# A long-convolution stage: split transforms against plain float32 transforms, and the order of a slot's two ways

## The chip, the cores and the metric

One core of one Trainium2 chip runs the whole program. The metric is the device time of one execution in microseconds (us). The kernel before took 4472.46 us (median of 3 runs, 4463.63 to 4475.19).

## What is computed

The program is two transformer blocks in float32 over 1024 positions and 1024 features. The change lies in the second block, in its Hyena branch:

```
z = v
for o, gate_o in enumerate((x1, x2)):
    z = gate_o * (bidirectional_long_conv(z, filters[:, o, 0], filters[:, o, 1]) + filt_bias[o] * z)
y_hy = z * jax.nn.silu(g_hy)

def bidirectional_long_conv(z, h_fwd, h_bwd):      # z: (B, L, C), h: (L, C), L = 1024
    circ = concatenate([h_fwd, zeros((1, C)), h_bwd[:0:-1]], axis=0)
    hf = rfft(circ, axis=0)
    zf = rfft(z, n=2 * L, axis=1)
    return irfft(zf * hf[None], n=2 * L, axis=1)[:, :L]
```

There are two convolutions in sequence over 512 channels, with filters that a small network makes. Beside them the second block has a wide input projection (`h @ w_in`), a windowed attention, and output projections.

## The kernel before, in words

**The transform.** A transform of length 2048 is made of two steps. A butterfly over 16 rows (8 of them zero for z) runs on VectorE (DVE) and GpSimd (POOL) in `dft16_even` and `dft16_odd`; it gives 8 *slots*, each a pair of tiles of 128x256 (real and imaginary part; the slots 0, 4, 2, 6 come from the even half, 1, 7, 3, 5 from the odd one). Then each slot is multiplied on TensorE (PE) with constant 128x128 matrices (`dft_mm`: four matrix products of 256 columns for a slot in each direction). The way back multiplies with the inverse matrices and ends in the butterfly `idft16`. Channels go in two groups g of 256, so with two orders o there are four convolutions of 8 slots.

**The split.** Before, a matrix product is three matmuls on float32r operands (a form of float32 rounded to fewer bits): `pair_split` (line 1318) rounds the pair on ScalarE (ACT, `pr_hi`, line 208) and makes the rest on POOL or DVE (`pr_lo`, line 214). The matrices, too, come in two parts; two big copies on POOL's DMA queue (`round_dft`, line 480, called in the first MLP of the program) put them into DRAM tiles of that type. Most large projections of the program (tiles `in`, `up`, `dn`) use such split products as well.

**The filter stage** (about 2864 to 3316 us). `filter_spectra` (line 1385) makes the spectra of the four filters, one call before each quarter of the projection to q, k and v: a small network (`f_ps`, plain float32 matmuls), butterflies, `flush` with 8 slots, each copied from PSUM by ACT (`spec`) and stored.

**The convolution stage** (about 3842 to 4234 us). `hyena` (line 1478) is a Python generator that yields; at 38 of its 56 yields `block2` puts in one *fill* step, 24 matmuls of the projection to the gates (tile `in`, `project_gate`). `long_conv` (line 1436) takes a slot through all of its steps: split, way there (`dft_ps`), load of the spectrum, product with the spectrum on DVE (`pt`, `pu`, lines 1456 to 1459, the last two halves on DVE or POOL), split again, a yield, way back (`idft_ps`), copy to the tile `V` by ACT. After eight slots `idft16` makes `conv_y`, the result is gated into z (`z<-conv_y,xgate`), there are four yields, and the next convolution begins with its butterflies. After each convolution of the second order, z is transposed on PE (`tp`, line 1504) and stored.

**What sets the order.** A scheduler merges the instructions into one queue for each engine, mostly as the program writes them; `high_priority` moves some ahead. An engine works its queue strictly in order. `lighter` (line 1193) puts an elementwise operation on DVE or POOL by a running sum of costs; `fma` is on DVE always. Tiles have a number of buffers (`bufs`), and a load waits on SyncE's (SP's) queue until its buffer is free.

Of the kernel before, what the change touches and what calls it, by code (L numbers as in the profile page):

```python
# [93 lines left out]
def _two_parts(x):  # L94

    def cut(v):
        m, e = np.frexp(v)
        return np.ldexp(np.rint(m * 4096), e - 12)

    hi = cut(x)  # L100
    return hi.astype(np.float32), cut(x - hi).astype(np.float32)


def _hyena_tables():
    f32 = np.float32
    c = {}
# [20 lines left out]
    for name, mats in (("dft_f", fwd), ("dft_i", inv)):  # L127
        parts = []
        for ms in mats:
            for m in ms:  # L130
                parts += list(_two_parts(m))
        c[name] = np.concatenate(parts, axis=1)
# [29 lines left out]
class Kernel:  # L162
# [317 lines left out]
    def round_dft(self, first):  # L480

        self.dft = {}
        for name in ("dft_f", "dft_i"):
            self.dft[name] = self.DR.tile([128, 50 * 128], F32R, name=name)
            self.in_order([first, self.nc.gpsimd.dma_start(self.dft[name], self.k[name])])

# [134 lines left out]
    def mlp(self, l, H, x, gate, p, close, pclose):  # L621
# [16 lines left out]
        def down_weights(c):  # L638
            dw = []
            for mt in range(2):  # L640
                n0 = c * 256 + mt * 128
                raw = pt.tile([128, 1024], F32, name="dn_raw", tag="dnr", bufs=2)
                nc.sync.dma_start(raw, down[n0 : n0 + 128, :])
                hi = p.tile([128, 1024], F32R, name="dn_hi", tag="dnh", bufs=3)
                lo = p.tile([128, 1024], F32R, name="dn_lo", tag="dnl", bufs=3)
                self.split_hi(hi, raw)
                first = self.split_lo(lo, raw, hi)
                if (l, c, mt) == (0, 4, 0):
                    self.round_dft(first)
                dw.append((hi, lo))  # L650
            return dw
# [603 lines left out]
    def idft16(self, p, v, n, y):  # L1255

        C1, C2, C3 = self.C1, self.C2, self.C3
        sub = ALU.subtract
        u = p.tile([128, 8, n], F32, name="bst", tag="bst", bufs=1)
        self.plus(u[:, 0:4], v[:, 0:4], v[:, 4:8])  # L1260
        self.plus(u[:, 4:8], v[:, 0:4], v[:, 4:8], sub)
        g = p.tile([128, 8, n], F32, name="bg", tag="bg", bufs=1)
        self.plus(g[:, 0:2], v[:, 8:10], v[:, 10:12])
        self.plus(g[:, 2:4], v[:, 8:10], v[:, 10:12], sub)
        self.plus(g[:, 4:6], v[:, 14:16], v[:, 12:14])
        self.plus(g[:, 6:8], v[:, 14:16], v[:, 12:14], sub)
# [10 lines left out]
        self.fma(y[:, 7], g[:, 1], C2, g[:, 5])  # L1277

# [16 lines left out]
    DFT_AT = {0: 0, **{d: 8 + 6 * (d - 1) for d in range(1, 8)}}  # L1295

    def dft_mats(self, p, which, d):
        n = 8 if d == 0 else 6
        m = p.tile([128, 8, 128], F32R, name="dftm", tag="dftm", bufs=2)
        at = self.DFT_AT[d] * 128  # L1300
        self.nc.sync.dma_start(m[:, :n].bitcast(F32).rearrange("p a b -> p (a b)"), self.dft[which].bitcast(F32)[:, at : at + n * 128])
# [16 lines left out]
    def pair_split(self, p, y, n):  # L1318
        hi = p.tile([128, 2, n], F32R, name="pr_hi", tag="pr_hi", bufs=2)
        lo = p.tile([128, 2, n], F32R, name="pr_lo", tag="pr_lo", bufs=2)  # L1320
        self.split_hi(hi, y)
        self.split_lo(lo, y, hi, True)
        return hi, lo
# [61 lines left out]
    def filter_spectra(self, p, o, g):  # L1385

        nc, n = self.nc, 256
        if o + g == 0:
            self.mats = p.tile([128, 50, 128], F32R, name="dftf")
# [22 lines left out]
        def flush(ds):  # L1412
            for d in ds:
                yy = self.pair_split(p, slots[d], n)
                if o + g == 0:
                    r = slice(self.DFT_AT[d], self.DFT_AT[d] + (6 if d else 8))
                    nc.sync.dma_start(self.mats[:, r].bitcast(F32).rearrange("p a b -> p (a b)"),
                                      self.dft["dft_f"].bitcast(F32)[:, r.start * 128 : r.stop * 128])
                ps = self.PS.tile([128, 2, n], F32, name="dft_ps", tag="sm", bufs=2)
                self.dft_mm(ps, self.mats[:, self.DFT_AT[d] :], yy, n, d)  # L1420
# [13 lines left out]
    V_AT = {0: (14, 15), 1: (0, 2), 2: (8, 9), 3: (1, 3), 4: (12, 13), 5: (5, 7), 6: (10, 11), 7: (4, 6)}  # L1434

    def long_conv(self, p, z, o, g):

        nc, n = self.nc, 256
        v = p.tile([128, 16, n], F32, name="V", tag="V", bufs=1)
        slots = {}  # L1440

        def Y(d):
            slots[d] = p.tile([128, 2, n], F32, name="Y", tag="Y", bufs=4)
            return slots[d]

        def through(ds):
            for d in ds:
                yy = self.pair_split(p, slots[d], n)
                m = self.dft_mats(p, "dft_f", d)
                ps = self.PS.tile([128, 2, n], F32, name="dft_ps", tag="sm", bufs=2)  # L1450
                self.dft_mm(ps, m, yy, n, d)
                h = p.tile([128, 3, n], F32, name="spec", tag="spec", bufs=1)
                nc.sync.dma_start(h, self.specd[o, g, d])
                t = p.tile([128, 2, n], F32, name="pt", tag="pt", bufs=1)
                u = p.tile([128, 2, n], F32, name="pu", tag="pu", bufs=1)
                nc.vector.tensor_mul(t, ps, h[:, 0:2])
                nc.vector.tensor_mul(u, ps, h[:, 1:3])
                self.plus(t[:, 0], t[:, 0], t[:, 1], ALU.subtract)
                self.plus(t[:, 1], u[:, 0], u[:, 1])
                gg = self.pair_split(p, t, n)  # L1460
                m = self.dft_mats(p, "dft_i", d)
                yield
                ps = self.PS.tile([128, 2, n], F32, name="idft_ps", tag="sm", bufs=2)
                self.dft_mm(ps, m, gg, n, d)
                a, b = self.V_AT[d]
                nc.scalar.activation(v[:, a : b + 1 : b - a], ps, AF.Copy)

        self.dft16_even(p, z, n, Y)
        yield
        yield from through((0, 4, 2, 6))  # L1470
        self.dft16_odd(p, z, n, Y)
        yield
        yield from through((1, 7, 3, 5))
        y = p.tile([128, 8, n], F32, name="conv_y", tag="conv_y", bufs=1)
        self.idft16(p, v, n, y)
        return y

    def hyena(self, hy, zd, xgd, yhd):
        nc, i = self.nc, self.i
# [6 lines left out]
        for o in range(2):  # L1486
            for g in range(2):
                ch = slice(g * 256, g * 256 + 256)
                y = yield from self.long_conv(hy, z[g], o, g)
                b = fb[:, o, ch].unsqueeze(1).to_broadcast([128, 8, 256])  # L1490
                for c in (slice(0, 4), slice(4, 8)):
                    self.plus(z[g][:, c], z[g][:, c], b[:, c], ALU.mult)
                    self.plus(y[:, c], y[:, c], z[g][:, c])
                for a in range(0, 8, 2):
                    gt = hy.tile([128, 2, 256], F32, name="xgate", tag="xgate", bufs=2)
                    nc.sync.dma_start(gt, xgd[o, a : a + 2, :, ch].rearrange("a p c -> p a c"))
                    self.plus(z[g][:, a : a + 2], y[:, a : a + 2], gt, ALU.mult)
                for _ in range(4):
                    yield
                for cc in range(2 if o else 0):  # L1500
                    for hf in range(2):
                        tp = self.PS.tile([128, 4, 128], F32, name="tp2", tag="sm", bufs=2)
                        for a in range(4):
                            nc.tensor.transpose(tp[:, a], z[g][:, 4 * hf + a, cc * 128 : cc * 128 + 128], self.ident)
                        t = hy.tile([128, 512], F32, name="zt", tag="zt", bufs=1)
                        nc.scalar.activation(t, tp.rearrange("p a b -> p (a b)"), AF.Copy)
                        nc.scalar.dma_start(yhd[2 * g + cc, hf], t)
# [37 lines left out]
    def block2(self, _, H, xs, close):  # L1545
# [45 lines left out]
        with self.pool("hyena", "right") as hy:  # L1591

            for n, _ in enumerate(self.hyena(hy, zd, xgd, yhd)):
                if (n + 1) * 38 // 56 > n * 38 // 56:
                    next(fill)
# [409 lines left out]
```

## Time and profile before

| | |
|---|---|
| median of 3 runs | 4472.46 us |
| the profiled execution | 4475.41 us, its span 4473.6 us |
| PE busy | 4130.8 us (92%) |
| DVE, ACT, POOL busy | 2082.0 (47%), 1488.5 (33%), 1488.1 us (33%) |
| DMA | 471.21 MB, mean 105 GB/s |
| mean granted clock of PE | 0.963 of full |

How to read it: a busy share is the time in which at least one instruction of the engine is in flight; matmuls overlap, so one of 392 ns can follow another after 228 ns. PEclk is the granted clock of PE as a share of the full 2.4 GHz; its other level is 0.5 (1.2 GHz). A plain float32 matmul stands in the trace as two records with the same names, a float32r one as one record. Waits are idle time of an engine ahead of an instruction, with the instruction that ended it.

### The profile page before, as it was taken

How to read it: one execution, taken by the hardware profiler on the slowest of the kernel's cores; microseconds unless marked ns; L12 is line 12 of the kernel's file. 1: busy time of each engine (PE TensorE's matmuls, PEld its weight loads, DVE VectorE, ACT ScalarE, POOL GpSimd, SP SyncE). 2: the span in 40 equal slices, each digit the busy share in tenths (PEclk: the TensorE clock that was granted, in tenths of full speed). 3: DMA queues.
4: the chain of work that ended last, by engine and by line, in shares of the span. 5: the costliest groups of instructions: out<-in, count | busy, mean ns of one | idle time of the engine just before them, and what ended most of it. 6: DMA issues, size and time to landing. Idle time of an engine off the chain costs nothing. (4 is left out here: it accounts for less than half of the span.)

```text
span 4473.6 us, 53257 instructions
## 1 busy us (share of the span) xinstructions
PE 4130.8 (92%) x20132; PEld 3220.5 (72%) x20132; DVE 2082.0 (47%) x3791; ACT 1488.5 (33%) x2822; POOL 1488.1 (33%) x1349
## 2 busy tenths in 40 slices
PE   6999888999999899888999999899999999877998
PEld 4776666888886686676888887567777676766777
DVE  6336675332335516586233324642322443577546
ACT  5435444212123515445212121323224444222222
POOL 3322455333333412254433332131230111355342
PEclk8999899999999999899999999999999999998999
DMA  6245533221111135623211111344453321645563
GB/s 195 62 134 164 166 121 92 92 61 52 47 51 58 47 106 180 202 93 116 74 44 52 43 52 48 105 123 104 113 145 83 90 86 48 188 150 157 164 193 113
DMA packets 566388, 471.21 MB, mean 105 GB/s; under 512 B 197416, under 2 KB 460670, under 8 KB 566002
## 3 DMA queue, kind: packets, MB, share of 16 engines
q1 hardware_dynamic: 375514, 367.43, 27.0%
q10 hardware_dynamic: 189880, 92.63, 7.2%
q0 software_dynamic: 736, 7.73, 0.5%
q8 instruction: 159, 2.61, 0.2%
q14 instruction: 99, 0.81, 0.1%
HBM read 364.17 MB, written 107.47 MB: 105 GB/s over the span
## 5 line engine op out<-in xcount | busy, mean ns | idle before, releaser
L214 POOL TENSOR_TENSOR w_lo<-w_raw,w_hi 128x1024 fp32r<-128x1024 f32 (+4 forms) x222 | 411.0, 1852 | 1015.8 <-ACT w_hi L208 936.4
L205 PE MATMUL dn<-act,dn_hi 128*128 128x512 f32 x2048 | 636.5, 392 | 9.8 <-ACT act L208 4.2
L662 DVE SCALAR_TENSOR_TENSOR xa<-dn,mod,xa 128x512 f32<-128x512 f32 x512 | 383.9, 750 | 277.8 <-PE dn L205 276.0
L205 PE MATMUL in<-b2h,w_hi 128*128 128x512 f32 x1152 | 467.3, 406 | 5.5 <-ACT qkv_t L1626 5.5
L205 PE MATMUL in<-b2h,w_lo 128*128 128x512 f32 x1152 | 466.6, 405 | 0.0
L205 PE MATMUL in<-b2l,w_hi 128*128 128x512 f32 x1152 | 466.3, 405 | 0.0
L208 ACT ACTIVATE w_hi<-w_raw 128x1024 fp32r<-128x1024 f32 (+4 forms) x276 | 236.8, 859 | 683.1 <-PE in L205 249.2
L205 PEld LDWEIGHTS dn<-act,dn_hi 128*128 128x128 f32 x2048 | 386.1, 189 | 95.1 <-ACT act L208 5.3
L205 PE MATMUL up<-fh,w_hi 128*128 128x512 f32 x1024 | 405.9, 396 | 0.7 <-DVE relu L632 0.4
L205 PE MATMUL up<-fl,w_hi 128*128 128x512 f32 x1024 | 402.9, 393 | 1.9 <-POOL fl L214 1.5
L205 PE MATMUL up<-fh,w_lo 128*128 128x512 f32 x1024 | 404.0, 395 | 0.0
L205 PE MATMUL dn<-act,dn_lo 128*128 128x512 f32 x1024 | 401.0, 392 | 2.8 <-POOL dn_lo L214 2.8
L632 DVE TENSOR_TENSOR relu<-up,relu 128x512 f32<-128x512 f32 x128 | 88.4, 691 | 604.5 <-ACT relu L631 604.5
L214 POOL TENSOR_TENSOR dn_lo<-dn_raw,dn_hi 128x1024 fp32r<-128x1024 f32 x64 | 151.9, 2392 | 524.5 <-ACT dn_hi L208 524.5
L205 PEld LDWEIGHTS in<-b2h,w_hi 128*128 128x128 f32 x1152 | 225.4, 196 | 57.4 <-issue 8.5
L205 PEld LDWEIGHTS in<-b2h,w_lo 128*128 128x128 f32 x1152 | 225.2, 195 | 51.6 <-issue 7.3
L205 PEld LDWEIGHTS in<-b2l,w_hi 128*128 128x128 f32 x1152 | 225.1, 195 | 50.0 <-issue 6.2
L208 ACT ACTIVATE dn_hi<-dn_raw 128x1024 fp32r<-128x1024 f32 x64 | 64.7, 1052 | 553.4 <-PE dn L205 546.1
L214 POOL TENSOR_TENSOR act<-relu,act 128x512 fp32r<-128x512 f32 x128 | 167.7, 1311 | 190.4 <-ACT act L208 190.3
L205 PEld LDWEIGHTS up<-fl,w_hi 128*128 128x128 f32 x1024 | 192.5, 188 | 49.0 <-POOL fl L214 3.2
L205 PEld LDWEIGHTS up<-fh,w_hi 128*128 128x128 f32 x1024 | 192.4, 188 | 46.6 <-issue 1.4
L205 PEld LDWEIGHTS up<-fh,w_lo 128*128 128x128 f32 x1024 | 192.6, 188 | 45.5 <-issue 1.0
(502 smaller groups left out, 8349.0 us busy)
## 6 DMA issues: line engine op xcount, KB each, us to landing
wada<-in_w_ada SPq DMA_DIRECT2D x120, 512.0 KB
w_raw<-in_w_in SPq DMA_DIRECT2D x102, 512.0 KB
w_raw<-in_w_mlp_up SPq DMA_DIRECT2D x64, 512.0 KB
dn_raw<-in_w_mlp_down SPq DMA_DIRECT2D x64, 512.0 KB
qkv<-qkv_t ACTq DMA_DIRECT2D x72, 256.0 KB
w_raw<-in_w_out SPq DMA_DIRECT2D x64, 256.0 KB
mix<-mix SPq DMA_DIRECT2D x64, 256.0 KB
spectra<-spec ACTq DMA_DIRECT2D x32, 384.0 KB
```

Of the source, the lines that this page charges most:

```text
L205: return self.nc.tensor.matmul(out, lhsT, rhs, start=start, stop=stop, **kw)
L208: self.nc.scalar.activation(hi, x, AF.Copy, **kw)
L214: return eng.tensor_sub(lo, x, hi.bitcast(F32))
L632: nc.vector.tensor_mul(sq, ps, sq)
L662: nc.vector.scalar_tensor_tensor(x[f, hf], ps, gate[:, f : f + 1], x[f, hf], op0=ALU.mult, op1=ALU.add)
```

## The change

1. Matrices and pairs are plain float32. `pair_split`, `round_dft` and the two-part matrices go; a product is one matmul, its matrix is loaded from the constants (192 KB in place of 384 KB for a slot).
2. `long_conv` goes. `hyena` runs over all 32 slots of the four convolutions in one sequence: way there of slot j (`slot_there`, with the product with the spectrum, all on DVE and at high priority), a yield, way back of slot j-1 (`slot_back`, with its own PSUM tag `im`). `idft16` is cut in two, the even half after four slots, the odd half after the first slot of the next convolution. The next convolution's butterflies are made while the slots of the present one run.
3. The fill steps are paced anew: 34 over the first 32 yields, then one at each. The buffers of matrices (2 to 5), spectra (1 to 2), `pt` (1 to 2) and slots (4 to 6) grow.

```diff
-    def dft_mm(self, ps, m, y, n, d):
-
-        yh, yl = y
+    def dft_mm(self, ps, m, y, d):
+
         if d == 0:
             terms = (((0, 0), (1, 1)), ((2, 0), (3, 1)))
         else:
             terms = (((0, 0), (2, 1)), ((1, 0), (0, 1)))
         for o in range(2):
-            k = 0
-            for mat, part in terms[o]:
-                for a, b in ((2 * mat, yh), (2 * mat, yl), (2 * mat + 1, yh)):
-                    self.mm(ps[:, o], m[:, a], b[:, part], k == 0, k == 5)
-                    k += 1
...
+            for k, (mat, part) in enumerate(terms[o]):
+                self.mm(ps[:, o], m[:, mat], y[:, part], k == 0, k == 1)
...
+    def slot_there(self, p, y, o, g, d):
...
+        m = self.dft_mats(p, "dft_f", d)
+        ps = self.PS.tile([128, 2, n], F32, name="dft_ps", tag="sm", bufs=2)
+        self.dft_mm(ps, m, y, d)
+        h = p.tile([128, 3, n], F32, name="spec", tag="spec", bufs=2)
+        nc.sync.dma_start(h, self.specd[o, g, d])
+        t = p.tile([128, 2, n], F32, name="pt", tag="pt", bufs=2)
+        u = p.tile([128, 2, n], F32, name="pu", tag="pu", bufs=1)
+        with self.tc.high_priority():
+
+            nc.vector.tensor_mul(t, ps, h[:, 0:2])
+            nc.vector.tensor_mul(u, ps, h[:, 1:3])
+            nc.vector.tensor_sub(t[:, 0], t[:, 0], t[:, 1])
+            nc.vector.tensor_add(t[:, 1], u[:, 0], u[:, 1])
+            self.load[0] += 0.84
+        return t, self.dft_mats(p, "dft_i", d)
+
+    def slot_back(self, p, t, m, v, d):
+
+        ps = self.PS.tile([128, 2, 256], F32, name="idft_ps", tag="im", bufs=2)
+        self.dft_mm(ps, m, t, d)
+        a, b = self.V_AT[d]
+        self.nc.scalar.activation(v[:, a : b + 1 : b - a], ps, AF.Copy)
...
+        for j in range(len(seq) + 1):
+            if j < len(seq):
+                k, half, at, d = seq[j]
+                on_way[j] = self.slot_there(hy, ready.pop((k, d)), *divmod(k, 2), d)
+            yield
+            if j == 0:
+                continue
+
+            k, half, at, d = seq[j - 1]
...
+            self.slot_back(hy, *on_way.pop(j - 1), V[half], d)
+            if (half, at) == (0, 0) and k:
+                self.idft16_odd(hy, V[1], n, y)
+                gating(k - 1, y)
+            if (half, at) == (0, 1):
+                self.dft16_odd(hy, z[k % 2], n, slots(k))
+            if (half, at, k) == (0, 2, 3):
+                features_first(0)
+            if (half, at) == (1, 0):
+                y = hy.tile([128, 8, n], F32, name="conv_y", tag="conv_y", bufs=1)
+                self.idft16_even(hy, V[0], n, y)
+            if (half, at) == (1, 1) and k < 3:
+                self.dft16_even(hy, z[1 - k % 2], n, slots(k + 1))
+        self.idft16_odd(hy, V[1], n, y)
+        gating(3, y)
+        for _ in range(3):
+            yield
+        features_first(1)
```

**The order on PE.** Between two slots, before in the first convolution and now at the start of the second (line 205 is the matmul helper, in the changed kernel line 191). Before:

```order
L205 MATMUL in_29577<-b2h_1_21970,w_hi 128x512
L205 MATMUL idft_ps<-pr_hi,dftm 128x256
L205 MATMUL in_29577<-b2l_1_21971,w_hi 128x512
L205 MATMUL in_29577<-b2h_1_21970,w_lo 128x512
L205 MATMUL dft_ps<-pr_hi,dftm 128x256
L205 MATMUL idft_ps<-pr_lo,dftm 128x256
L205 MATMUL idft_ps<-pr_hi,dftm 128x256 x2
L205 MATMUL idft_ps<-pr_lo,dftm 128x256
```

and now, one row with x4 being all products of a slot in one direction:

```order
L191 MATMUL in_29254<-b2l_1_21977,w_hi 128x512
L191 MATMUL in_29254<-b2h_1_21976,w_lo 128x512
L191 MATMUL idft_ps<-pt,dftm 128x256 x4
L191 MATMUL dft_ps<-Y,dftm 128x256 x4
L191 MATMUL in_29355<-b2h_0_21701,w_hi 128x512
L191 MATMUL in_29355<-b2l_0_21702,w_hi 128x512
```

Before, the first `pr_hi` matmul of a slot stands ahead of its `pr_lo` ones, and fill and two slots mix. Now all four products of one slot's way back stand together with the next but one slot's way there, and 24 fill matmuls stand between such visits.

**The order on DVE.** From the first convolution into the second (`z_29048`, now `z_28660`, is z of the first channel group, `z_29050`, now `z_28662`, of the second; lines 1204 and 1208 are elementwise helpers, now 1181 and 1185; 1418 to 1421 are the product with the spectrum; 1677, now 1675, ends a gate). Before:

```order
L1204 TENSOR_TENSOR conv_y<-conv_y,bst 128x256
L1208 SCALAR_TENSOR_TENSOR conv_y<-bpq,conv_y 128x256 x12
L1204 TENSOR_TENSOR bst<-z_29050 128x1024
L1677 SCALAR_TENSOR_TENSOR gate_t<-in_29842,b_in,gate_t 128x512
L1204 TENSOR_TENSOR conv_y<-conv_y,z_29048 128x1024
L1204 TENSOR_TENSOR z_29048<-conv_y,xgate 128x512
L1204 TENSOR_TENSOR Y<-bst 128x512
L1204 TENSOR_TENSOR Y<-bst 128x256
L1204 TENSOR_TENSOR bmn<-bst 128x256 x2
L1208 SCALAR_TENSOR_TENSOR Y<-bmn,bst 128x256
L1677 SCALAR_TENSOR_TENSOR gate_t<-in_29957,b_in,gate_t 128x512
L1208 SCALAR_TENSOR_TENSOR Y<-bmn,bst 128x256
```

and now:

```order
L1185 SCALAR_TENSOR_TENSOR conv_y<-bpq,conv_y 128x256 x5
L1418 TENSOR_TENSOR pt<-dft_ps,spec 128x512
L1419 TENSOR_TENSOR pu<-dft_ps,spec 128x512
L1420 TENSOR_TENSOR pt<-pt 128x256
L1181 TENSOR_TENSOR conv_y<-conv_y,z_28660 128x1024
L1421 TENSOR_TENSOR pt<-pu 128x256
L1181 TENSOR_TENSOR z_28660<-conv_y,xgate 128x512
L1181 TENSOR_TENSOR bpq<-z_28662 128x256 x5
L1185 SCALAR_TENSOR_TENSOR bst<-bpq,z_28662 128x256 x2
L1675 SCALAR_TENSOR_TENSOR gate_t<-in_29355,b_in,gate_t 128x512
L1181 TENSOR_TENSOR z_28660<-conv_y,xgate 128x512
L1185 SCALAR_TENSOR_TENSOR bst<-bpq 128x256 x2
```

Before, the next convolution's first slots (`Y`) come behind the whole way out of the last one (`conv_y`, `z`). Now that way out stands between the spectrum products of the next convolution's first slots, and ahead of the butterflies of its odd half (`bpq<-z`).

## Rows read from the trace of the kernel before

**Rows 1.** View of stretches: start:end, length, busy us (instructions) of each engine

```profile
core 0: us, PE busy (x) PEld busy (x) DVE busy (x) ACT busy (x) POOL busy (x), PEclk, DMA share, GB/s
870.00:890.00 20.00, 20.00 (x89) 16.37 (x88) 3.77 (x6) 5.42 (x7) 8.30 (x6) 1.00 0.67 234
2864.00:3316.00 452.00, 418.57 (x1849) 326.94 (x1848) 168.32 (x268) 127.47 (x263) 129.30 (x84) 0.95 0.43 120
3842.20:4233.80 391.60, 321.93 (x1666) 265.37 (x1667) 267.21 (x400) 99.52 (x155) 191.76 (x135) 0.91 0.53 164
```

**Rows 2.** The same view, at a change of convolution and at the stage's end

```profile
3900.00:3950.00 50.00, 35.96 (x175) 29.27 (x173) 39.08 (x51) 9.19 (x14) 30.50 (x22) 0.86 0.45 139
...
4215.00:4230.00 15.00, 6.56 (x24) 4.50 (x23) 6.69 (x3) 2.83 (x4) 7.25 (x4) 0.66 0.49 155
```

**Rows 3.** Waits of TensorE (PE), convolution stage: us in total, times, longest us

```profile
PE dft_ps L205 <- ACT pr_hi L208: 22.9, 2, 11.5
PE tp L1504 <- POOL z L1204: 20.6, 4, 11.1
PE idft_ps L205 <- ACT pr_hi L208: 11.7, 11, 2.7
```

**Rows 4.** Waits of PE, filter stage, 2864 to 3316 us

```profile
PE dft_ps L205 <- POOL pr_lo L214: 13.7, 9, 4.5
PE dft_ps L205 <- ACT pr_hi L208: 8.4, 5, 3.8
```

**Rows 5.** View of stretches for tile `in` alone, convolution stage: the projection's matmuls

```profile
3842.20:4233.80 391.60, 218.86 (x866) 162.89 (x867) 7.43 (x10) 24.39 (x36) 0.91 0.53 164
```

**Rows 6.** Groups of PE in the convolution stage: shapes, count | busy us, mean ns

```profile
L205 PE MATMUL dft_ps<-pr_hi,dftm 128*128 128x256 f32 x256 | 57.9, 304 | 28.9 <-ACT pr_hi L208 22.9 <-DMA dftm<-dft_f 5.9
...
L1504 PE MATMUL tp<-ident,z 128*128 128x128 f32 x32 | 7.5, 356 | 22.8 <-POOL z L1204 20.6 <-DVE z L1204 2.2
```

**Rows 7.** Timeline of PE, 4195 to 4200 us: start us, length us, engine, line, tiles, count

```profile
4195.28 0.40 PE L205 MATMUL in<-b2l,w_hi 128*128 128x512 f32 x1
...
4197.79 0.39 PE L205 MATMUL in<-b2h,w_hi 128*128 128x512 f32 x1
...
4199.15 0.40 PE L205 MATMUL idft_ps<-pr_hi,dftm 128*128 128x256 f32 x2
...
4200.34 0.39 PE L205 MATMUL in<-b2l,w_hi 128*128 128x512 f32 x1
```

**Rows 8.** Timeline of PE, 2837 to 2845 us: plain float32 matmuls of 512 columns

```profile
2837.45 7.13 PE L205 MATMUL ms<-nsq,ones_d 128*128 128x512 f32 x16
...
2844.65 0.39 PE L205 MATMUL in<-b2h,w_lo 128*128 128x512 f32 x1
```

**Rows 9.** Timeline of PE, 2998 to 3003 us: plain float32 matmuls of 256 columns

```profile
2998.10 4.95 PE L205 MATMUL f_ps<-fw,fhid 64*128 64x256 f32 x20
3002.98 0.50 PE L205 MATMUL in<-b2h,w_hi 128*128 128x512 f32 x1
```

**Rows 10.** Timeline of VectorE (DVE), 3914 to 3956 us: from one convolution into the next

```profile
3914.67 1.23 DVE L1204 TENSOR_TENSOR bst<-V 128x1024 f32<-128x1024 f32 x1 [2.62 <-ACT V L1466]
...
3922.74 6.30 DVE L1208 SCALAR_TENSOR_TENSOR conv_y<-bpq,conv_y 128x256 f32<-128x256 f32 x12
...
3930.76 2.70 DVE L1204 TENSOR_TENSOR conv_y<-conv_y,z 128x1024 f32<-128x1024 f32 x1
3933.39 2.83 DVE L1204 TENSOR_TENSOR z<-conv_y,xgate 128x512 f32<-128x512 f32 x1
...
3944.64 2.43 DVE L1204 TENSOR_TENSOR bpq<-z 128x256 f32<-128x256 f32 x3
...
3954.62 0.74 DVE L1208 SCALAR_TENSOR_TENSOR Y<-bst 128x256 f32<-128x256 f32 x2
```

**Rows 11.** Groups of GpSimd (POOL) in the convolution stage

```profile
L214 POOL TENSOR_TENSOR pr_lo<-Y,pr_hi 128x512 fp32r<-128x512 f32 x30 | 45.3, 1509 | 97.2 <-ACT pr_hi L208 88.8 <-DMA dftm<-dft_f 5.0 <-DMA spec<-spectra 3.4
```

**Rows 12.** Groups of DVE in the convolution stage

```profile
L1456 DVE TENSOR_TENSOR pt<-dft_ps,spec 128x512 f32<-128x512 f32 x32 | 22.0, 688 | 39.4 <-PE dft_ps L205 37.7 <-issue 1.4
```

More of the change, by code (lines that the diff above doesn't have):

```diff
@@ L127, in _hyena_tables @@
     for name, mats in (("dft_f", fwd), ("dft_i", inv)):
[L128 to L132, printed above, removed]
+        c[name] = np.concatenate([m for ms in mats for m in ms], axis=1).astype(np.float32)
     L, E, bands = S, 33, 16
@@ L646, in down_weights @@
                 self.split_hi(hi, raw)
-                first = self.split_lo(lo, raw, hi)
-                if (l, c, mt) == (0, 4, 0):
-                    self.round_dft(first)
+                self.split_lo(lo, raw, hi)
                 dw.append((hi, lo))
@@ L1277, in idft16, with idft16_odd @@
         self.fma(y[:, 7], g[:, 1], C2, g[:, 5])
+    def idft16_odd(self, p, v, n, y):
+        C1, C2, C3 = self.C1, self.C2, self.C3
+        sub = ALU.subtract
+        u = p.tile([128, 8, n], F32, name="bst", tag="bst", bufs=1)
+        self.plus(u[:, 0:4], v[:, 0:4], v[:, 4:8])
+        self.plus(u[:, 4:8], v[:, 0:4], v[:, 4:8], sub)
         w = p.tile([128, 6, n], F32, name="bpq", tag="bpq", bufs=1)
@@ L1293, in idft16 @@
                 self.fma(y[:, b], w[:, a - 1], sg * cp, y[:, b])
-    DFT_AT = {0: 0, **{d: 8 + 6 * (d - 1) for d in range(1, 8)}}
+    DFT_AT = {0: 0, **{d: 4 + 3 * (d - 1) for d in range(1, 8)}}
     def dft_mats(self, p, which, d):
-        n = 8 if d == 0 else 6
-        m = p.tile([128, 8, 128], F32R, name="dftm", tag="dftm", bufs=2)
+        n = 3 if d else 4
+        m = p.tile([128, 4, 128], F32, name="dftm", tag="dftm", bufs=5)
         at = self.DFT_AT[d] * 128
-        self.nc.sync.dma_start(m[:, :n].bitcast(F32).rearrange("p a b -> p (a b)"), self.dft[which].bitcast(F32)[:, at : at + n * 128])
+        self.nc.sync.dma_start(m[:, :n].rearrange("p a b -> p (a b)"), self.k[which][:, at : at + n * 128])
         return m
-    def dft_mm(self, ps, m, y, n, d):
-        yh, yl = y
+    def dft_mm(self, ps, m, y, d):
         if d == 0:
@@ L1432, in filter_spectra @@
         flush((1, 7, 3, 5))
-    V_AT = {0: (14, 15), 1: (0, 2), 2: (8, 9), 3: (1, 3), 4: (12, 13), 5: (5, 7), 6: (10, 11), 7: (4, 6)}
-    def long_conv(self, p, z, o, g):
+    V_AT = {0: (6, 7), 1: (0, 2), 2: (0, 1), 3: (1, 3), 4: (4, 5), 5: (5, 7), 6: (2, 3), 7: (4, 6)}
+    def slot_there(self, p, y, o, g, d):
         nc, n = self.nc, 256
[L1439 to L1476, printed above, removed]
@@ L1485, in hyena @@
             nc.sync.dma_start(z[g], zd[g].rearrange("a p c -> p a c"))
[L1486 to L1507, printed above, removed]
@@ new lines, in hyena, with slots, Y, gating @@
+        ready = {}
+        def slots(k):
+            def Y(d):
+                ready[k, d] = hy.tile([128, 2, n], F32, name="Y", tag="Y", bufs=6)
+                return ready[k, d]
+            return Y
+        def gating(k, y):
+            o, g = divmod(k, 2)
+            ch = slice(g * 256, g * 256 + 256)
+            b = fb[:, o, ch].unsqueeze(1).to_broadcast([128, 8, 256])
+            for c in (slice(0, 4), slice(4, 8)):
+                self.plus(z[g][:, c], z[g][:, c], b[:, c], ALU.mult)
+                self.plus(y[:, c], y[:, c], z[g][:, c])
+            for a in range(0, 8, 2):
+                gt = hy.tile([128, 2, 256], F32, name="xgate", tag="xgate", bufs=2)
+                nc.sync.dma_start(gt, xgd[o, a : a + 2, :, ch].rearrange("a p c -> p a c"))
+                self.plus(z[g][:, a : a + 2], y[:, a : a + 2], gt, ALU.mult)
@@ new lines, in features_first @@
+        def features_first(g):
+            for cc in range(2):
+                for hf in range(2):
+                    tp = self.PS.tile([128, 4, 128], F32, name="tp2", tag="sm", bufs=2)
+                    for a in range(4):
+                        nc.tensor.transpose(tp[:, a], z[g][:, 4 * hf + a, cc * 128 : cc * 128 + 128], self.ident)
+                    t = hy.tile([128, 512], F32, name="zt", tag="zt", bufs=1)
+                    nc.scalar.activation(t, tp.rearrange("p a b -> p (a b)"), AF.Copy)
+                    nc.scalar.dma_start(yhd[2 * g + cc, hf], t)
@@ new lines, in hyena @@
+        self.dft16_even(hy, z[0], n, slots(0))
+        seq = [(k, half, at, d) for k in range(4) for half, ds in enumerate(((0, 4, 2, 6), (1, 7, 3, 5))) for at, d in enumerate(ds)]
+        V, y, on_way = {}, None, {}
+        for j in range(len(seq) + 1):
[6 more added lines that the diff above has]
+            k, half, at, d = seq[j - 1]
+            if at == 0:
+                V[half] = hy.tile([128, 8, n], F32, name=f"V{half}", tag=f"V{half}", bufs=1)
+            self.slot_back(hy, *on_way.pop(j - 1), V[half], d)
[11 more added lines that the diff above has]
+                self.dft16_even(hy, z[1 - k % 2], n, slots(k + 1))
@@ L1593, in block2 @@
             for n, _ in enumerate(self.hyena(hy, zd, xgd, yhd)):
-                if (n + 1) * 38 // 56 > n * 38 // 56:
+                if n >= 32 or (n + 1) * 34 // 32 > n * 34 // 32:
+                    next(fill)
+                if n < 32 and (n + 1) * 34 // 32 > n * 34 // 32 + 1:
                     next(fill)
```

44 lines of the change are left out of this document (11 added, 33 removed).

## Prediction

> **What bounds the kernel now.** I read the view of stretches first. In the convolution stage TensorE (PE) is busy 321.9 of 391.6 us, DVE 267.2 and POOL 191.8 [rows 1]: PE bounds, but stands idle for 69.7 us, and its mean granted clock is 0.91, so about 18% of the stage went at the lower of the two levels, half speed. In the filter stage it is busy 418.6 of 452.0 us at 0.95 [rows 1]. The idle time is not spread evenly. Where one convolution gives way to the next, PE is busy 36.0 of 50 us while DVE is busy 39.1, and at the stage's end 6.6 of 15 us at a clock of 0.66 [rows 2]. The waits say for what: 22.9 us in only two waits for `pr_hi` of a new convolution's slot, 20.6 us for the finished z ahead of the transposes, 11.7 us in small waits for `pr_hi` between the two ways of a slot [rows 3]. In the filter stage it is the split again, 13.7 us for `pr_lo` and 8.4 us for `pr_hi` [rows 4].
>
> How much is to be had? PE's work without any wait has a floor. 866 fill matmuls [rows 5] follow one another after (4197.79 - 4195.28) / 11 = 0.228 us [rows 7]: 197.4 us. A float32r matmul of 256 columns takes (4200.34 - 4199.15) / 10 = 0.119 us [rows 7]; a slot has 12 in each direction, 768 in all (256 of them in the row shown, [rows 6]): 91.4 us. With the transposes' 7.5 us [rows 6] the floor is 296.3 us. So 391.6 - 296.3 = **95.3 us** of this stage are waits and half speed. The change can win there, and nowhere else as much.
>
> **The products themselves** get dearer. A plain float32 product is two records in the trace. Sixteen of 512 columns and one fill matmul fill 7.20 us [rows 8], so a record takes (7.20 - 0.23) / 16 = 0.436 us, and of 256 columns half, 0.218: 0.436 us for a product, against 3 x 0.119 = 0.357 before. The other bound are records of 256 columns that use only 64 rows of the array: 4.88 / 20 = 0.244 us [rows 9], 0.488 for a product. I take 0.436, from full 128x128 matrices like these. The 256 products of the convolutions then take 111.6 us in place of 91.4, +20.2 us. Entering a run of plain products costs some 0.1 us more ([rows 9] stand 0.5 us above 20 x 0.218; with four records to an entry that is five entries); 33 visits: +3.3 us. Page "FP8 and Floating Point Precision" of the Trainium skill, section "TensorE Precision Notes", says that true float32 takes four passes through the array. By that a product would be an estimated 4 x 0.119 = 0.476 us, 15.4 us more over all 384 products than by my price; [rows 8] lie below it and are nearer to this use.
>
> **The order** pays for that. What is late next? Between the two ways of a slot now stand another slot's products and 24 fill matmuls, 5.5 us, against a spectrum product of four DVE instructions (0.69 us for each of the two wide ones [rows 12], some 2.2 us together): the small waits go, and `pr_hi`, `pr_lo` go with the split. At a change of convolution the way out of the old one (`idft16_odd`, gating) now runs under the new one's even slots, whose `Y` were made during the old one. Late next are then the odd slots. Their chain on DVE is: `bst` to the end of `conv_y`, 3914.67 to 3929.0, 14.4 us; gating, 2.70 + 2.83 = 5.5 us; butterflies from `bpq` to the first odd `Y`, 3944.64 to 3955.4, 10.7 us [rows 10]; two spectrum products, 4.4 us. That is 35.0 us. But these DVE instructions ran beside a busy POOL at up to twice their usual length (the twelve `conv_y` here 0.52 us apart; the same width costs 0.37 us in the last of [rows 10]), and POOL loses 45.3 us of `pr_lo` [rows 11]. I take 30 us. The cover is three slot steps from the last way back to the first odd way there, each 24 x 0.228 + 8 x 0.436 + 0.1 = 9.1 us: 27 us. So 3 us of waiting stay at each of three changes, and some 2 us of half speed behind them: 15 us. At the start the first four slots stand close together with little fill between them, after a wait for z that stays: 8 us. At the end the last way out (14.4 + 5.5 us) has three fill steps of 16.4 us as cover: 4 us of waiting and 4 of half speed. Together 31 us of the 95.3 stay.
>
> Convolution stage after: 296.3 + 20.2 + 3.3 + 31 = 350.8 us, against 391.6: **-41 us**.
>
> **The filter stage.** 128 products, each 0.079 dearer: +10 us, and some 24 entries, +2. The 22.1 us of waits for the split [rows 4] have no split to wait for any more; but slots stand closer together now, and the DVE butterflies feed them, so I count three quarters, 17 us, as gone: **-5 us**. Bounds: +12 with nothing won, -20 with all of it and the half speed behind it.
>
> **What costs nothing.** The two copies of `round_dft` go; PE was busy 20.00 of the 20 us around them [rows 1], so nothing waited. ACT loses 96 `pr_hi`, and is no bound at 99.5 us. DVE gains the spectrum product's last halves that POOL shared, and loses its share of `pr_lo`; at 267 of 391.6 us [rows 1] it has room. On SP's queue the matrices stand behind the gating's loads (`xgate`), which wait for z; with five buffers they are two and a half slots, 22 us, ahead, more than the gating's 5.5 us. Matrix loads halve; the waits for them are not among those shown. POOL's queue holds `w_lo` of the fill between butterflies, as before. If that cover fails, odd slots come later, which is the third rival.
>
> **Sum.** -41 - 5 = -46 us on the profiled execution's 4475.4 us (span 4473.6); it stands 3 us above the median of the runs, so **4427 us**. A measurement tells no change from one within 0.3%, 13 us.
>
> **Rivals.**
> - *All waits go* (14%). DVE's instructions shorten to their undisturbed length, the chain falls to 25 us and is covered, the filter stage gives 20 us: 4427 - 15 - 5 - 15 = 4392 us. For it: DVE loses work and POOL 45 us. Against it: start and end stay as they are.
> - *The dear product* (10%): a product costs 0.488 us, as in [rows 9], 384 x 0.052 = +20 us: 4447 us. Against it speaks [rows 8]. By the four passes of the Trainium skill's page it would be an estimated 4442 us.
> - *The butterflies take the wait's place* (5%, slower). DVE works in order, and the spectrum products, put ahead, hold up the butterflies whenever PE is late, while the way out waits for POOL's half of `bst<-V`, queued behind a `w_lo`. Each us of the chain beyond 27 costs 3 us, once per change. From a chain of 50 us on, the kernel is slower than the bound; at 52 us it gives 4427 + 3 x 22 + 3 = 4496 us. Before, the chain with a busy POOL was 35.0 us [rows 10], so much more than that is needed.
> - *No difference* (9%): the dear product, the chain at its full 35.0 us with 12 us lost at each change (+21), together 4427 + 20 + 21 = 4468 us. That the way back does not stand behind the next slot is excluded by the order on PE.
>
> **How the numbers follow.** The forecast keeps 62%. Its own range, 4408 to 4446, is the chain between 27 and 33 us and the filter stage's bounds. The range of 8 in 10 reaches down to the first rival, 4392, and up to 4460, where the no-difference case begins. Faster by over 13 us: forecast, first and second rival, 0.86; same 0.09; slower 0.05.
>
> **What would show it.** In the profile after: two records of about 0.22 us pitch for a product, 512 records each for `dft_ps` and `idft_ps` in the stage; its length near 351 us; PE's waits for `pr_hi` and `pr_lo` gone, small waits for `Y` at the first odd slot of a convolution, a wait for z of some 4 us before the last transposes; PEclk up from 0.91 towards 0.96. It is wrong if PE waits more than 10 us for `Y` at each change, if records lie 0.24 us apart, or if the stage of attention or the end moves, where PE's order is the same.

## The result and the profile after

The changed kernel takes **4432.24 us** (median of 4 runs, 4425.2 to 4444.01), the kernel before 4469.45 us in runs on the same chip: a ratio of 0.9919, 95% interval 0.9894 to 0.9945. A second measurement gave 0.992 (0.990 to 0.9941). The forecast was 4427 us. The profiled execution of the changed kernel is the slowest of its four, 4444.01 us with a span of 4442.2 us, so the two traces differ by 31 us, the medians by 37.

The view of stretches of the changed kernel: start:end, length, busy us (instructions) of each engine, PEclk, DMA share, GB/s. First the convolution stage, then the stretch from the last score product of the attention to the last transpose, then six us behind a wait.

```profile
3843.10:4202.80 359.70, 325.91 (x1414) 272.18 (x1415) 238.56 (x373) 64.06 (x92) 150.98 (x98) 0.94 0.46 143
...
3769.30:4202.60 433.30, 394.12 (x1748) 327.88 (x1748) 258.73 (x403) 85.21 (x124) 165.60 (x107) 0.95 0.45 139
...
3951.70:3957.70 6.00, 6.00 (x14) 4.78 (x15) 6.00 (x11) 0.00 (x0) 1.41 (x2) 0.51 0.63 200
```

The convolution stage fell from 391.6 us [rows 1] to 359.7, PE's idle time in it from 69.7 to 33.8 us, and PEclk rose from 0.91 to 0.94. What is left of the waits (waits of PE in the stage: us in total, times, longest us; the last of them, for a load, ends at the stage's first product and so lies just ahead of it):

```profile
PE dft_ps L191 <- issue: 16.4, 2, 11.2
PE tp L1467 <- DVE pu L1419: 6.7, 1, 6.7
PE idft_ps L191 <- DVE pt L1420: 4.4, 1, 4.4
PE tp L1467 <- DVE z L1181: 3.4, 2, 2.2
PE tp L1467 <- POOL z L1181: 2.7, 2, 2.0
PE dft_ps L191 <- DMA dftm<-const_dft_f: 2.6, 1, 2.6
```

Nothing waits for `pr_hi` or `pr_lo` any more [rows 3]. The two waits whose releaser is not named (11.2 and 5.2 us) stand ahead of the first odd slot of the second and of the third convolution. DVE shows what they were: the matmul follows the start of its `Y` by half a microsecond at both (3951.70 after 3951.19, 4036.78 after 4036.26). The timeline of DVE at the first:

```profile
3919.54 0.43 DVE L1185 SCALAR_TENSOR_TENSOR bpq<-bst 128x256 f32<-128x256 f32 x1 [2.28 <-POOL bst L1181]
...
3922.64 2.58 DVE L1185 SCALAR_TENSOR_TENSOR bpq<-bst 128x256 f32<-128x256 f32 x1
...
3930.49 0.68 DVE L1418 TENSOR_TENSOR pt<-dft_ps,spec 128x512 f32<-128x512 f32 x1
...
3943.04 2.88 DVE L1185 SCALAR_TENSOR_TENSOR bst<-bpq 128x256 f32<-128x256 f32 x2
3945.84 2.89 DVE L1185 SCALAR_TENSOR_TENSOR bst<-bpq,z 128x256 f32<-128x256 f32 x2
...
3951.19 2.75 DVE L1185 SCALAR_TENSOR_TENSOR Y<-bst 128x256 f32<-128x256 f32 x8
```

and the timelines of PE and of POOL (same columns):

```profile
3867.27 1.89 PE L191 MATMUL idft_ps<-pt,dftm 128*128 128x256 f32 x8
3869.00 1.89 PE L191 MATMUL dft_ps<-Y,dftm 128*128 128x256 f32 x8
3876.19 1.89 PE L191 MATMUL idft_ps<-pt,dftm 128*128 128x256 f32 x8
...
3951.70 3.75 PE L191 MATMUL dft_ps<-Y,dftm 128*128 128x256 f32 x8 [11.23 <-issue]
```

```profile
3914.59 4.92 POOL L1181 TENSOR_TENSOR bst<-V 128x1024 f32<-128x1024 f32 x2 [8.16 <-ACT V L1430]
...
3922.40 2.54 POOL L200 TENSOR_TENSOR w_lo<-w_raw,w_hi 128x1024 fp32r<-128x1024 f32 x1
...
3930.38 2.41 POOL L1181 TENSOR_TENSOR conv_y<-conv_y,z 128x1024 f32<-128x1024 f32 x1 [5.44 <-DVE conv_y L1185]
...
3942.52 3.12 POOL L1181 TENSOR_TENSOR bg<-V 128x512 f32<-128x512 f32 x2
3945.60 2.52 POOL L200 TENSOR_TENSOR w_lo<-w_raw,w_hi 128x1024 fp32r<-128x1024 f32 x1
```

Eight records take 3869.00 - 3867.27 = 1.73 us, so a plain product of two records takes 0.432 us. A slot step takes 3876.19 - 3867.27 = 8.92 us. The chain from `bst` (on POOL now) to the first odd `Y` takes 3951.5 - 3914.6 = 37 us, and PE had work for 26 of them. After the wait PE works at the lower level of its clock for 6 us (0.51), in the other rows of the stage it is mostly at the higher.

**Where the 31 us of the two traces come from.** I cut both at the same four instructions. The first cut is a sum ahead of the filter stage (`ms<-nsq`, at 2837.45 us [rows 8] and 2850.29), behind the same PE work in both. Up to it: +12.8 us; from there to the first score product of the attention (the filter stage): 560.8 to 548.4, **-12.4**; attention: 366.7 to 370.7, +4.0; from the last score product to the last transpose: 468.7 to 433.3, **-35.4**; the rest: -0.4. The filter stretch in four kernels, two with the split (before, and `order_alone` below) and two without (changed, and `odd_first` below):

```profile
2837.45:3398.24 560.79, 521.82 (x2282) 409.20 (x2281) 190.39 (x294) 166.35 (x342) 139.86 (x89) 0.95 0.44 119
...
2841.24:3396.40 555.16, 513.72 (x2284) 403.61 (x2283) 192.59 (x294) 166.58 (x342) 140.95 (x89) 0.97 0.45 121
...
2850.29:3398.64 548.35, 518.89 (x2154) 406.06 (x2153) 164.41 (x275) 148.89 (x310) 105.19 (x76) 0.97 0.44 117
...
2848.79:3396.40 547.61, 517.75 (x2156) 405.84 (x2155) 164.41 (x275) 148.61 (x310) 105.16 (x76) 0.97 0.44 117
```

Over all profiles of this study it takes 555.1 to 560.8 us in the four kernels with the split and 547.1 to 548.7 in the ten profiles without: the filter stage did gain. But half or more of that is lost just ahead of it. The last stretch of the first block (from its last 128 `dn` matmuls to `ms<-nsq`) takes 64.3 to 66.2 us with the split and 70.0 to 71.7 without. PE's order differs there. Before, `dn` follows the last `ms<-nacc`; now the block's last five `up` matmuls stand between them:

```profile
2809.94 2.03 PE L205 MATMUL ms<-nacc,ones_d 128*128 128x512 f32 x2 [2.89 <-POOL nacc L1541]
2810.98 1.84 PE L205 MATMUL dn<-act,dn_hi 128*128 128x512 f32 x2
...
2815.26 2.08 PE L191 MATMUL ms<-nacc,ones_d 128*128 128x512 f32 x2 [1.10 <-POOL nacc L1537]
2816.35 1.42 PE L191 MATMUL up<-fl,w_hi 128*128 128x512 f32 x1
```

Why the scheduler orders it so, and whether that order is what costs the time, was not tried. The attention has the same work in both, and over the profiles of this study it took 354 to 373 us: its +4.0 is the spread of single executions. The gain that stays is nearly all the convolution stage's.

### The profile page after: what moved, and what is told of

The parts are those of the page before. It is cut to its first block, busy times and chain, and to the rows that moved or that the text cites. A ratio compares the mean times of both kernels' runs of the same rounds, so it can differ in the third digit from the quotient of the medians.

```text
span 4442.2 us, 52202 instructions
## 1 busy us (share of the span) xinstructions
PE 4143.3 (93%) x19748; PEld 3232.0 (73%) x19748; DVE 2024.9 (46%) x3742; ACT 1434.8 (32%) x2726; POOL 1416.9 (32%) x1300
## 5 line engine op out<-in xcount | busy, mean ns | idle before, releaser
L200 POOL TENSOR_TENSOR w_lo<-w_raw,w_hi 128x1024 fp32r<-128x1024 f32 (+4 forms) x236 | 445.4, 1888 | 1119.4 <-ACT w_hi L194 1027.7
L194 ACT ACTIVATE w_hi<-w_raw 128x1024 fp32r<-128x1024 f32 (+4 forms) x276 | 236.8, 859 | 749.3 <-PE in L191 316.3
L191 PEld LDWEIGHTS dn<-act,dn_lo 128*128 128x128 f32 x1024 | 194.1, 190 | 44.9 <-POOL dn_lo L200 3.6
```

Source lines behind the costliest of these rows:

```text
L191: return self.nc.tensor.matmul(out, lhsT, rhs, start=start, stop=stop, **kw)
L194: self.nc.scalar.activation(hi, x, AF.Copy, **kw)
L200: return eng.tensor_sub(lo, x, hi.bitcast(F32))
```

## The experiments

For each kernel, "stretch" is the time from the last score product to the last transpose in its profile (before 468.7 us with PE idle for 77.6; changed 433.3 with 39.2). It begins ahead of the stage, since in some of these kernels the stage's first slots are interleaved with the attention's last work. "The order" in the runs below includes the change's new pacing of the fill, which no run tries by itself.

### The plain products alone

```diff
 # the kernel before, dft_mm, dft_mats and filter_spectra as in the change
-                yy = self.pair_split(p, slots[d], n)
...
-                gg = self.pair_split(p, t, n)
```

> The kernel before, in its own order, with the plain float32 products of the change and without the splits. Theory (the order brings the gain of the convolution stage): the filter stage shortens by about 12 us as in the changed kernel (its code is the same), and in the convolution stage 20 to 25 us of dearer products eat most of the 35 us of waits for the split, since each slot's way back still waits for its own spectrum product: stage 380 to 392 us, whole 4445 to 4460 us. Rival (the gain comes from dropping the split, in whatever order): stage about 360 us, whole about 4432 us, as the changed kernel. A third: the dear products dominate, stage over 400 us, whole above 4465 us.

Measured: 4449.72 us, ratio 0.9946 (0.9928 to 0.9964); stretch 451.6 us. The whole time is as the theory had it. In its profile the filter stretch shortened by 13.7 us (560.8 to 547.1), much as expected, and the stretch by 17.1, while the rest of the program took some 3 us more. The waits of PE in its convolution stage:

```profile
PE idft_ps L191 <- POOL pt L1181: 19.8, 13, 14.3
PE tp L1467 <- POOL z L1181: 14.5, 4, 8.7
PE dft_ps L191 <- POOL Y L1181: 7.8, 1, 7.8
```

The waits for `pr_hi` [rows 3] go without any new order. That is worth more than the dearer products cost: PE's idle time in the stretch falls by 23.1 us (77.6 to 54.5), and its busy time rises by only 6.0 (391.1 to 397.1) instead of 20, at a granted clock of 0.94 in place of 0.92.

### The order alone

```diff
 # the changed kernel, dft_mm and the matrices as in the kernel before
-        self.dft_mm(ps, m, y, d)
+        self.dft_mm(ps, m, self.pair_split(p, y, n), n, d)
...
-        return t, self.dft_mats(p, "dft_i", d)
+        return self.pair_split(p, t, n), self.dft_mats(p, "dft_i", d)
```

> The order of the change with the three float32r products of the split, of the kernel before, in both stages (matrices in two buffers and one buffer of spectra, for want of room). Theory (order): the filter stage stays at its 563 us, and the convolution stage falls to 345 to 370 us, 20 us less of products than the changed kernel but with ACT's and POOL's splits back between the spectrum product and the way back, which the next slot's way there now hides: whole 4425 to 4450 us. Rival (dropping the split is what counts): waits for the split's high and low part come back, stage 385 us or more, whole 4465 us or more.

Measured: 4486.81 us, ratio 1.0032 (1.0021 to 1.0043), slower than before by 0.3%; stretch 485.8 us. PE waited 44.1 us there for loads of matrices, since only two buffers had room: no fair trial of the order. This kernel and the next two also keep one buffer of `pt` and of spectra, where the change has two. With three buffers of matrices:

> The order of the change with the split products, as in order_alone, but with three buffers of matrices instead of two (the first slot's two extra matrices in a tile of their own; five buffers of Y instead of six pay for it). In order_alone TensorE waited 44.1 us for the loads of matrices. From the last score product of the attention to the last transpose the stretches are 468.8 us in the kernel before, 451.5 with the plain products alone, 433.3 in the changed kernel. Theory (order and plain products each take a part of the waits): the loads' waits go, stretch 440 to 452 us, whole 4437 to 4455 us. Rival (under this order the split itself is on the path: POOL's low parts queue behind butterflies on POOL): stretch 455 to 470 us, whole 4455 to 4475 us.

Measured: 4482.37 us, ratio 1.002 (1.0007 to 1.0034); stretch 481.4 us. The rival came out, and more: the loads' waits went, and the split's came in their place.

```profile
PE dft_ps L205 <- POOL pr_lo L214: 43.4, 24, 5.1
```

As written, the split of slot j+1's `Y` stands behind the split of slot j's spectrum on ACT and POOL, so the way there of j+1 waits for the whole way of j's data: the order hides little. So I wrote it earlier:

```diff
         self.dft_mm(ps, m, y, n, d)
+        ahead()                    # the split of slot j+1, in its own pair of buffers
```

> order_alone_3bufs with the split of the next slot's Y written ahead of the spectrum product of this slot, in a pair of buffers of its own, so that on ACT and POOL it no longer stands behind the split of the spectrum. In order_alone_3bufs TensorE waited 43.4 us in 24 waits for POOL's low part ahead of the way there. Theory (that place in the written order is what cost the order its gain): those waits go, the stretch from the last score product to the last transpose falls from 481.4 us to 435 to 455 us, whole 4435 to 4455 us. Rival (POOL, with splits and butterflies, is late in any order): stretch 465 us or more, whole 4465 us or more.

Measured: 4461.54 us, ratio 0.9987 (0.9971 to 1.0003); the profiled execution is the fastest of its ten, 4446.03 us, with a stretch of 453.8 us. It lies 15.5 us below the median; outside the stretch it took 3990.5 us, the least of all profiles here (the others take up to 4013.8), so a part of the 15.5 us lies there, and a part may lie in the stretch. `pr_lo` holds the way there for 10.1 us instead of 43.4:

```profile
PE dft_ps L205 <- ACT pr_hi L208: 15.5, 3, 5.9
PE idft_ps L205 <- POOL pr_lo L214: 11.3, 6, 2.7
PE dft_ps L205 <- POOL pr_lo L214: 10.1, 3, 4.4
```

So the place of the split cost the order alone a good part of what it lost (the two intervals of the ratio do not overlap); the profile's stretch is in the theory's range, the median between theory and rival. By the ratios the products alone give 24 us, the order alone costs 9 us as written and gives some 6 us (-1 to 13, so perhaps nothing) with the split early, both together 36. The two parts are not a sum: the plain product is dearer for PE, and it takes the split out of the order's way.

### What the priority does

```diff
-        with self.tc.high_priority():
```

> The changed kernel without the higher priority of the spectrum product, so that VectorE may run butterflies that were written earlier ahead of it. Theory (a slot's way back has some 7 us of cover, the next way there and the fill, and a burst of butterflies is 8 to 30 us): waits of TensorE for pt come at the four or more bursts, 10 to 40 us in all, whole 4443 to 4470 us. Rival (the scheduler places it in time anyhow, or the waits only change place with those for the odd slots): 4425 to 4438 us.

> The changed kernel unaltered, beside the other runs of this call, to tell their differences from the chip's. All theories: 0.9895 to 0.9945 of the kernel before, about 4433 us.

Measured: without the priority 4434.86 us, 0.9921 (0.990 to 0.9943), stretch 433.4 us; the changed kernel beside it 4438.61 us, 0.992. The rival: the priority gives nothing.

### The chain at a change of convolution

```diff
-            if (half, at) == (0, 0) and k:
-                self.idft16_odd(hy, V[1], n, y)
-                gating(k - 1, y)
-            if (half, at) == (0, 1):
-                self.dft16_odd(hy, z[k % 2], n, slots(k))
+            if (half, at) == (0, 0):
+                self.dft16_odd(hy, z[k % 2], n, slots(k))
+            if (half, at) == (0, 1) and k:
+                self.idft16_odd(hy, V[1], n, y)
+                gating(k - 1, y)
```

> The changed kernel with the odd half of the transform there written ahead of the odd half of the transform back and the gating at each change of convolution. Theory (what is left of TensorE's idle time is that chain of 37 us against 27 us of cover): the waits of 11.2 and 5.2 us ahead of the first odd slot go, with part of the half speed behind them: convolution stage 337 to 347 us, whole 4410 to 4420 us. Rival (the same work only comes later: the gated input of the next convolution but one, or the last slots, wait in its place): stage 355 to 365 us, whole 4427 to 4440 us.

Measured: 4420.66 us, 0.9879 (0.9851 to 0.9907), stretch 420.6 us, PE idle in it for 25.8 us in place of 39.2. Repeated:

> odd_first unaltered, for a narrower interval of the version that has been fastest. All theories: 0.986 to 0.990 of the kernel before, about 4422 us, below the changed kernel's 0.990 to 0.994.

Measured: 4424.81 us, 0.9898 (0.9878 to 0.9917), stretch 421.1 us. The theory: the 16.4 us of waits ahead of odd slots are gone, and the stage, 347.1 us, and the whole time are at the upper end of the forecast. The largest waits of PE that stay in it:

```profile
PE idft_ps L191 <- DVE pt L1421: 5.5, 2, 3.4
PE tp L1467 <- POOL z L1181: 5.0, 2, 3.2
PE dft_ps L191 <- DMA dftm<-const_dft_f: 3.9, 1, 3.9
```

Two moves of fill on top of it:

```diff
-                if n < 32 and (n + 1) * 34 // 32 > n * 34 // 32 + 1:
+                if n in (0, 31):
...
-        for _ in range(3):
+        for _ in range(4):
```

> odd_first with two small moves of fill: one of the two extra portions stands at the first slot instead of the sixteenth, and one more portion stands ahead of the last transposes. odd_first keeps 5.5 us of waits for pt (the first slot) and 5.0 us for the gated z ahead of the last transposes. Theory (TensorE's idle time there is filled and its clock kept): 5 to 10 us less than odd_first, 0.986 of the kernel before, 4405 to 4416 us. Rival (the fill was free there anyway and is missed where it is taken away): 4417 to 4424 us, as odd_first.

Measured: 4425.43 us, 0.9904 (0.9882 to 0.9926). The stretch fell once more, to 411.3 us, but the whole time did not follow in six runs: no difference that these runs show.

### Is PE the bound?

```diff
-            for k, (mat, part) in enumerate(terms[o]):
+            for k, (mat, part) in enumerate(terms[o][:1]):
```

> The changed kernel with one of each two products of the convolution stage left out, there and back, so that its transforms are incomplete (128 products of 0.43 us, 55 us of TensorE's work, go). Theory A (TensorE bounds the stage but for the changes of convolution): the stage falls by 30 to 50 us, to 310 to 330 us, and the waits for butterflies grow by the rest. Theory B (VectorE's butterflies set the pace already): it falls by less than 20 us, to 340 us or more.

Measured in a single execution: 4388.38 us; stage 316.6 us, 43 less. PE's work in the stretch fell by 52.0 us (394.1 to 342.2, 0.41 us for each product), its idle time rose by 9, and the unnamed waits ahead of odd slots grew from 16.4 to 27.6 us:

```profile
3758.00:4148.20 390.20, 342.16 (x1491) 280.60 (x1492) 258.88 (x403) 83.69 (x124) 169.61 (x107) 0.93 0.49 154
```

```profile
PE dft_ps L191 <- issue: 27.6, 3, 12.5
```

Theory A: PE bounds the stage; only at the changes does DVE.

### Who stretches the chain?

The chain was 37 us where 30 were forecast. In the timelines above a DVE instruction of 0.41 us takes 2.58 us while POOL's `w_lo` runs, and four others take 1.44 us each beside `bg` and `w_lo`. So POOL's share was taken away:

```diff
     def lighter(self, cost_vector=0.62, cost_pool=1.23):
         load = self.load
-        if load[1] + cost_pool <= load[0] + cost_vector:
+        if not getattr(self, "alone", False) and load[1] + cost_pool <= load[0] + cost_vector:
...
+        self.alone = True          # in hyena, ahead of its first butterfly; False behind its last gating
```

> The changed kernel with every butterfly and gating instruction of the convolution stage on VectorE, none on GpSimd (which keeps the low parts of the fill's weights). In the changed kernel the chain at the first change of convolution took 37 us; a 256-wide instruction with both inputs in SBUF took 2.58 us there in place of 0.41 beside one of GpSimd. Theory (the two engines hold each other up, so that GpSimd's share does not shorten the chain): VectorE's busy time rises by less than 50 us, the waits ahead of the first odd slots (11.2 and 5.2 us) do not grow, stretch from the last score product to the last transpose 425 to 438 us, whole 4425 to 4437 us. Rival (GpSimd's share is real relief): VectorE becomes the bound, waits of TensorE grow by 15 us or more, whole 4450 us or more.

> odd_first with every butterfly and gating instruction of the convolution stage on VectorE. Theory (the engines hold each other up): the stretch stays at its 421 us or falls by up to 8, whole 4412 to 4424 us. Rival (GpSimd's share is real relief): stretch 435 us or more, whole 4435 us or more.

Measured: 4394.12 us, **0.9829** (0.981 to 0.9848), for the changed kernel with all of it on DVE, and 4396.35 us, 0.9826 (0.9805 to 0.9848), for `odd_first` with it. Far more than the theory had. The low parts of the fill's weights, which go by the same chooser, moved to DVE too (14 of 16 `w_lo`), against what was expected of the edit. The convolution stage of the first, from the view of stretches (columns as above), its last waits of PE (the 3.9 us lie ahead of its first product), and three groups of DVE (shapes, count | busy us, mean ns):

```profile
3829.80:4147.70 317.90, 314.31 (x1412) 264.08 (x1413) 228.90 (x467) 64.18 (x92) 4.76 (x2) 1.00 0.51 159
```

```profile
PE dft_ps L191 <- DVE Y L1181: 3.9, 1, 3.9
PE tp L1467 <- DVE z L1181: 2.0, 2, 1.8
PE dft_ps L191 <- issue: 1.5, 2, 1.0
```

```profile
L1418 DVE TENSOR_TENSOR pt<-dft_ps,spec 128x512 f32<-128x512 f32 x32 | 22.1, 690 | 26.0 <-PE dft_ps L191 25.9
...
L1420 DVE TENSOR_TENSOR pt<-pt 128x256 f32<-128x256 f32 x32 | 13.4, 419 | 0.0
...
L1185 DVE SCALAR_TENSOR_TENSOR bpq<-bst 128x256 f32<-128x256 f32 x16 | 6.3, 421 | 0.0
```

The same groups in the changed kernel:

```profile
L1418 DVE TENSOR_TENSOR pt<-dft_ps,spec 128x512 f32<-128x512 f32 x32 | 21.9, 683 | 48.7 <-PE dft_ps L191 48.7
...
L1420 DVE TENSOR_TENSOR pt<-pt 128x256 f32<-128x256 f32 x32 | 19.8, 619 | 0.0
...
L1185 DVE SCALAR_TENSOR_TENSOR bpq<-bst 128x256 f32<-128x256 f32 x16 | 12.4, 820 | 4.6 <-POOL bst L1181 4.6
```

DVE does 94 instructions more and is busy for *less*: 228.9 us in place of 238.6, while POOL's 151.0 us shrink to 4.8. PE is idle for 3.6 us of 317.9, with its clock at the higher level nearly all through. The chain at the first change of convolution (timeline of DVE) is 30 us long and ends as PE comes to need it (last row, timeline of PE):

```profile
3895.89 1.23 DVE L1181 TENSOR_TENSOR bst<-V 128x1024 f32<-128x1024 f32 x1 [1.04 <-ACT V L1430]
...
3925.92 2.77 DVE L1185 SCALAR_TENSOR_TENSOR Y<-bst 128x256 f32<-128x256 f32 x8
...
3926.44 1.97 PE L191 MATMUL dft_ps<-Y,dftm 128*128 128x256 f32 x8 [0.53 <-issue]
```

With that, writing the odd half first has nothing left to win: 0.9826 and 0.9829 are the same. What the moved `w_lo` alone brings, and whether the kernel before would win as much without POOL, wasn't tried.

## Why the prediction came out right, and where it did not

- **PE bounds the stage, and its waits are the room**: right. Leaving out half of the products took 43 of some 52 us off the stage. The room was 95.3 us; after the change 43 are left (the stage's 359.7 less 870 fill matmuls at 0.228, 256 products at 0.432 and the transposes' 7.3, 316.3 us), where the prediction left 31. PEclk rose to 0.94, short of the 0.96 that was named.
- **The product at 0.436 us**: right, 0.432 measured. By the four passes that the Trainium skill's page "FP8 and Floating Point Precision", section "TensorE Precision Notes", names, it would have been an estimated 0.476. The measurement decides against that estimate, which takes a whole float32r step of 0.119 us for each pass; how many passes there are no run here shows. The dear product of the rivals, 0.488 us, is out by the measurement too. The 0.1 us for an entry does not show: 24 fill matmuls at 0.228 and 16 records at 0.216 make 8.93 us, and the slot step took 8.92. The sum had 3.3 us for it. "512 records each" was a slip: 512 is the sum of the two, 256 each.
- **"The order pays for that"**: the step that failed as an attribution. The small waits were put down to the order. Dropping the split alone won 17 us of the stretch net of the dearer products; the order alone, with the split, lost 13, and only with the split rewritten did its stretch win (15 us, in a profile that may flatter it). The sum held because both parts were made together.
- **The changes of convolution**: right mechanism, wrong size. Chain 37 us against a forecast of 30, cover as forecast (a slot step of 8.92 us against 9.1). Waits 11.2, 5.2 and none, 16.4 us in place of 9. The forecast took POOL's load on DVE to fall away with `pr_lo`; it did not. Without POOL's share the chain is the 30 us of the forecast, though two `w_lo` of 1.2 us stand in it now.
- **Start and end**: 7.0 us of waits at the start (4.4 for `pt`, and 2.6 for a load just ahead of the stage) against 8; 6.1 at the end against 4 of waiting. What no term had: 6.7 us ahead of the first transposes, which now stand between slots and wait for `pu`, since their PSUM tag is that of `dft_ps` (read from the program; no run tried another tag).
- **Filter stage**: right in direction, sized too small: -12.4 us in the pair of traces against -5 forecast. PE's idle time there fell from 39.0 to 29.5 us, and its busy time did not rise by the 12 us of dearer products and entries (521.8 to 518.9, at a granted clock of 0.97 in place of 0.95).
- **A term that the sum did not have**: the end of the first block, whose PE order the change moved as well, takes 6.5 us more in the pair of traces. In the whole time it hides half of what the filter stage gave.
- **Sum**: 37 us in the medians against 46. The convolution stage gave 32 in place of 41, the filter stage 12 in place of 5, and the first block took some back. That 4432 lies only 5 us from 4427 is in part luck: the kernel before came out 3 us lower here than the median from which the forecast counted.
- **The rivals**: butterflies do take the wait's place, but the chain is far from the 50 us at which that decides. "All waits go" named DVE at its undisturbed length as its condition and 4392 us as its time; the kernel that makes the condition true takes 4394. That the two times agree so well is in part luck: the rival leaves some 331 us for the convolution stage, and this kernel's takes 317.9, since most waits at the start and the end went too.

## What to carry to other kernels

Ask of each operation that is shared out to a second engine whether the first gets faster by it: a group's mean duration with and without a neighbour tells, and here giving POOL nothing was worth as much again as the whole change. A dearer operation can be the cheaper one when it takes two engines out of the path between two matmuls. And an order that hides latency is only as good as the queues it is written into: the same order lost time while one split stood behind another. And when two traces are cut into stages, cut them at an instruction with the same work ahead of it in both: at another sum of the first block, which PE's new order had moved, the filter stage's gain would have looked like 5 us in place of 12.

## What the runs showed of the hardware

GpSimd can hold a VectorE instruction up by more than the factor of two that the prediction allowed: 2.58 us for 0.41 in one instance, which ends 0.3 us after POOL's instruction does. Not every instruction suffers. `pt<-dft_ps`, with one input in PSUM, keeps its length (683 ns beside POOL's work, 690 without; 0.68 us in the middle of POOL's 2.41 us of `conv_y`); `pt<-pt`, with both in SBUF, goes from a mean of 419 to 619 ns, `bpq<-bst` from 421 to 820. The Trainium skill's page "SBUF — State Buffer", section "Who interferes with whom", has this rule: a VectorE instruction with two inputs in SBUF contends with a GpSimd instruction that reads SBUF, and one with at most one SBUF input, outside the two-port modes, does not. The trace agrees in both halves. What that makes of a whole stage is shown by VectorE's own busy time: 146 us of work moved from GpSimd to VectorE, and VectorE was busy for 9.7 us less.
